# The order of vector and scalar work behind the seven value products, and who forms the rests of one pair's weights

## The chip, the cores and the metric

The kernel runs on one core of a Trainium2 chip. A core has TensorE (PE, matrix products, which land in the accumulation banks "PSUM"), VectorE (DVE), ScalarE (ACT), GpSimd (POOL) and SyncE (SP, which here only issues DMAs). Each engine works through its own queue strictly in order and waits at an instruction until its inputs are there. The metric is the device time of one execution in microseconds, the median of several.

## The reference

A two-layer encoder over 512 tokens of width 1024. The change lies in layer 0, neighbourhood attention on a grid 64 tokens wide:

```python
q, k, v, z = jnp.split(xn @ w_in, 4, axis=-1)      # xn: 512 x 1024, w_in: 1024 x 4096
o = neighbourhood_attention(q, k, v, rpb)          # 16 heads of 64, window 8 x 16, softmax
return (o.reshape(B, S, hd) * jax.nn.silu(z)) @ w_out
```

After it come a gated embedding, layer 1 (latent attention with its own gate) and a final norm. All is float32.

## The kernel before

**Two parts for one number.** A float32 matrix product is made of three passes on rounded parts: an operand is copied by ACT into `whi` (or `xh`, `da`, ...), rounded to the matmul's format, and its rest, operand minus copy, goes into `wlo` (`xl`, `la`, ...). PE then adds hi x hi, hi x lo and lo x hi. A weight of 128 x 1024 (`wraw`, loaded by a DMA that SyncE issues) thus costs one ACT copy and one subtraction, the "rest". `load_w` lets POOL form the rest in one operation of 128 x 1024; `piece` lets DVE form it in two halves of 128 x 512 (`rest`). Both draw on the same rings of three buffers for `wraw`, `whi` and `wlo`.

**Seven products for the values.** `values_seven` computes v = xn @ w_v (512 x 1024 x 1024) by Strassen's scheme in Winograd's form: 2 x 2 blocks and seven products instead of eight, in the order 1, 2, 7, 6, 5, 4, 3. Each product is 24 matmuls of 128 x 512, in two row blocks i = 0, 1 and two depths c = 0, 1, with two weight pieces `W[p][c]`. Products 7, 6, 5, 3 take mixed inputs `V7`, `V6`, `V5`, `V3` (DVE forms the sum into `xT`, ACT its `hi`, DVE its `lo`: `mix`). The mixed weights come from DMAs that add in flight (`W7`, `W5`: `load`) and from sums on DVE (`sums`: `W7` plus a raw piece, in place). Products 5 and 3 add into the banks `C[6]` of product 6, product 4 into the banks `C[7]` of product 7. Between products DVE and ACT combine banks: `after7` adds the saved product 1 (`s1`) to `C[7]` and saves that as `s17`; `after6` saves `C[6]` as `s6` and subtracts it from `C[7]`; `after5` forms the difference of `C[6]` and `s17` and that of `C[6]` and `s1`. `out` splits a finished bank into the tiles `Q` that the attention reads. A bank that is still to be read by a copy or a subtraction cannot be added to by the next product.

**Two head pairs in between.** The query and key projections of head pairs 0 and 1 are set among the seven products (`Pair`): `load` fetches the two weights, `products` runs 2 x 24 matmuls into the "mm" banks, `queries` makes `sa`, `sb` of the first bank, `keys` makes `da`, `db` (ACT) and the rests `la`, `lb` (DVE) of the second, and then the edge copies `s0` on ACT. There are two "mm" banks, so pair 1's products need that `queries(0)` and `keys(0)` have read pair 0's. All later pairs are made by `project`, one before each pair's attention.

**What sets the order.** In this stretch `self.act` and `self.dve` are wrapped in `InOrder`, so that ACT and DVE run in exactly the order in which the lines of `values_seven` stand. PE's value products and pair products are chained likewise. The matmuls of attention heads, of `project` and of all later stages are placed by a planner at build time. POOL and SyncE take their instructions in the planner's order too. Helpers called through `InOrder` are recorded under L51 in the profile.

Of the kernel before, what the change touches and what calls it, by code (L numbers as in the profile page):

```python
# [13 lines left out]
F32 = mybir.dt.float32  # L14
F32R = mybir.dt.float32r
AF = mybir.ActivationFunctionType
ALU = mybir.AluOpType
AX = mybir.AxisListType
PSUM = bass.MemoryType.PSUM
P = 128  # L20
# [36 lines left out]
class Trunk:  # L57
# [189 lines left out]
    def rest(self, hi, lo, raw, o):  # L247
        return self.dve.tensor_tensor(out=lo[:, o], in0=raw[:, o], in1=hi[:, o].bitcast(F32), op=ALU.subtract)
# [18 lines left out]
    def values_seven(self, pool, xT, xk, Q, pair, more):  # L267

        nc = self.nc
        quarter = lambda n, c: self.a["na_v"][n, c:c + 2].rearrange("c p n -> p c n")  # L270
        T = {}

        def load(p, n, c):
            T[p] = pool.tile([P, 2, 1024], F32, name=f"W{p}", bufs=1)
            nc.sync.dma_start(T[p], quarter(1, 0))
            nc.gpsimd.dma_start(T[p], quarter(n, c), accum_op=ALU.add, max_dma_last_dim=4096)

        load(7, 1, 2)
        W, X, C, s1, s17, s6 = {}, {}, {}, {}, {}, {}
        sums = lambda t, i, raw: self.dve.tensor_tensor(out=t[:, i, :], in0=t[:, i, :], in1=raw, op=ALU.add)  # L280

        def left(p, s, k, i):
            if p in X:
                return X[p][:, 2 * s + k // 2, k % 2 * 256 + i * P:k % 2 * 256 + (i + 1) * P]
            half, t = {1: (0, i), 2: (1, i), 4: (1, 2 + i)}[p]
            return xT[s][half][:, k, t * P:(t + 1) * P]

        banks = {1: "SS", 7: "TT", 6: "TO"}
        base = {2: 1, 4: 7, 5: 6, 3: 6}

        def product(p):
            for i in range(2):
                if p in banks:
                    C[p, i] = self.psum(banks[p][i])
            for c, i in [(0, 0), (0, 1), (1, 0), (1, 1)] if p in (1, 2, 7) else [(0, 0), (1, 0), (0, 1), (1, 1)]:
                ps = C[base.get(p, p), i]
                m = [(left(p, s, k, i), W[p][c][r][:, k % 2 * S:(k % 2 + 1) * S])
                     for s, r in ((0, 0), (1, 0), (0, 1)) for k in (2 * c, 2 * c + 1)]
                for j, (l, r) in enumerate(m):
                    with self.tc.issue_after(self.last_mm.ins):  # L300
                        self.last_mm = nc.tensor.matmul(ps, l, r, start=c == 0 and j == 0 and p in banks,  # L301
                                                        stop=c == 1 and j == 5 and p in (2, 3, 4),
                                                        skip_group_check=True)

        sub = lambda o, x, y: self.dve.tensor_tensor(out=o, in0=x, in1=y, op=ALU.subtract)
        kept = lambda name, i: self.temp(name) if name == "s1" or (name, i) == ("s17", 0) else pool.tile([P, S], F32, name=name, tag="s", bufs=3)

        def copy(name, i, ps):
            t = kept(name, i)
            self.act.activation(t, ps, AF.Copy)  # L310
            return t

        def out(th, n, i, ps):
            self.v_split(Q[th, n][:, 2 * i:2 * i + 2, :], ps)

        def after1(i):
            s1[i] = copy("s1", i, C[1, i])

        def after7(i):
            self.dve.tensor_tensor(out=C[7, i], in0=C[7, i], in1=s1[i], op=ALU.add)  # L320
            s17[i] = copy("s17", i, C[7, i])

        def after6(i):
            s6[i] = copy("s6", i, C[6, i])
            sub(C[7, i], C[7, i], s6[i])

        def after5(i):
            q = self.psum("mm")
            sub(q, C[6, i], s17[i])
            sub(C[6, i], C[6, i], s1[i])  # L330
            out(1, 1, i, q)

        made = lambda p, c, raw, vw=False: W.setdefault(p, []).append(self.piece(pool if vw else None, raw)())
        both = range(2)

        def mixed(p):
            X[p], rest = self.mix(xk, p)
            return rest

        made(1, 0, self.raw_piece(0, 0))  # L340
        rest7 = mixed(7)
        made(1, 1, self.raw_piece(0, 1), True)
        load(5, 0, 0)
        rest7()
        made(2, 0, self.raw_piece(0, 2))
        pair.products(0)
        pair.queries(0)
        rest5 = mixed(5)
        product(1)
        after1(0)  # L350
        p21 = self.piece(None, self.raw_piece(0, 3))
        after1(1)
        rest5()
        W[2].append(p21())
        pair.load(1)
        rest6 = mixed(6)
        rest3 = mixed(3)
        rest6()
        rest3()
        more()  # L360
        pair.keys(0)
        made(7, 0, T[7][:, 0, :], True)
        product(2)
        out(0, 0, 0, C[1, 0])
        out(0, 0, 1, C[1, 1])
        made(7, 1, T[7][:, 1, :])
        raws = [self.raw_piece(0, c) for c in both]
        sums(T[7], 0, raws[0])
        made(6, 0, T[7][:, 0, :], True)
        sums(T[7], 1, raws[1])  # L370
        pair.products(1)
        pair.queries(1)
        made(6, 1, T[7][:, 1, :])
        raws = [self.raw_piece(0, 2 + c) for c in both]
        pair.keys(1)
        sums(T[7], 0, raws[0])
        sums(T[7], 1, raws[1])
        made(5, 0, T[5][:, 0, :])
        product(7)
        made(4, 0, T[7][:, 0, :], True)  # L380
        after7(0)
        after7(1)
        made(5, 1, T[5][:, 1, :])
        product(6)
        after6(0)
        after6(1)
        made(4, 1, T[7][:, 1, :], True)
        made(3, 0, self.raw_piece(1, 2))
        product(5)
        made(3, 1, self.raw_piece(1, 3))  # L390
        after5(0)
        after5(1)
        product(4)
        out(1, 0, 0, C[7, 0])
        out(1, 0, 1, C[7, 1])
        product(3)
        out(0, 1, 0, C[6, 0])
        out(0, 1, 1, C[6, 1])

    def na_heads(self, pool, xT, zs, Q, xk, weights, more):  # L400
        nc, a = self.nc, self.a
        A, U = {}, {}
# [18 lines left out]
        def edges(q, last):  # L421
            s0 = []
            for s in q:
                e0 = pool.tile([P, P], F32R, name="s0", tag="s0", bufs=4)
                with self.tc.issue_after(last.ins):
                    self.act.activation(e0.rearrange("p (a b) -> p a b", a=2),
                                        win(s, 0, P, 0, [[448, 2], [1, 64]]).bitcast(F32), AF.Copy)
                s0.append(e0)
            return s0

        def keys(j, psk):
            da = pool.tile([P, S], F32R, name="da", tag="kd", bufs=4)
            db = pool.tile([P, S], F32R, name="db", tag="kd", bufs=4)
            la, lb = self.rest_k[j % 2]
            self.act.activation(da[0:64], psk[0:64], AF.Copy)
            self.act.activation(da[64:128], psk[0:64], AF.Copy)
            self.act.activation(db[64:128], psk[64:128], AF.Copy)
            self.last_key = self.act.activation(db[0:64], psk[64:128], AF.Copy)
            self.dve.tensor_tensor(out=la[0:64], in0=psk[0:64], in1=da[0:64].bitcast(F32), op=ALU.subtract)
            self.dve.tensor_tensor(out=lb[64:128], in0=psk[64:128], in1=db[64:128].bitcast(F32), op=ALU.subtract)  # L440
            return (da, db), (la, lb)

        class Pair:
            ps = {}

            @staticmethod
            def load(j):
                weights[j] = [self.load_w(a["na_qk"][i + j], 1024) for i in (0, 8)]

            @staticmethod  # L450
            def products(j):
# [8 lines left out]
            @staticmethod  # L460
            def keys(j):
                k = keys(j, Pair.ps[j][1])
                A[j] += (edges(A[j][0], self.last_key), *k)

        def project(j):
            wq = self.load_w(a["na_qk"][j], 1024)
            psq = self.psum("mm")
            self.proj_T(psq, wq, xT)
            q = queries(psq)
            wk = self.load_w(a["na_qk"][8 + j], 1024)  # L470
            psk = self.psum("mm")
            last = self.proj_T(psk, wk, xT)
            k = keys(j, psk)
            A[j] = (q, edges(q, self.last_key), *k)
            return last

# [16 lines left out]
        for i in range(2):  # L493
            la = pool.tile([P, S], F32R, name=f"la{i}", bufs=1)
            lb = pool.tile([P, S], F32R, name=f"lb{i}", bufs=1)
# [10 lines left out]
        with self.tc.tile_pool(name="nah", bufs=2, reuse_waits="tile") as hpool:  # L506
            for j in range(8):
                if 0 < j < 7:
                    last = project(j + 1)
                l, step = divmod(j, 4)  # L510
# [948 lines left out]
```

## Time and profile before

| | |
|---|---|
| median of 3 runs | 661.22 us (660.08 to 661.79) |
| the profiled execution | 661.75 us, of which the span of the trace is 660.0 us |
| mean granted clock of TensorE | 0.988 |
| instructions | 9977 |
| POOL's share of the span | 63% |
| DMA | 107.41 MB in all, mean 163 GB/s |

The page cuts the span into 40 slices of 16.5 us, a digit being tenths of a slice in which the engine is busy. The value products run from 55 us to 115 us, that is in slices 4 to 7; the sixteen heads of layer 0 follow up to about 280 us. The profile names tiles without their numbers: `ps_T`, `ps_O`, `ps_S` and `ps_mm` are banks, `s` stands for `s1`, `s17`, `s6` and also for `s0`, `W` for `W7` and `W5`, `V` for all mixed inputs.

### The profile page before, as it was taken

The numbers are of one execution on the slowest core, as the hardware profiler recorded it, in microseconds if no ns is written. First come the engines' busy times: TensorE is split into PE (matmuls) and PEld (weight loads), VectorE is DVE, ScalarE is ACT, GpSimd is POOL, SyncE is SP. The second block draws the span as 40 slices with busy tenths as digits, with TensorE's granted clock in tenths as the row PEclk, the third lists the DMA queues.
The fourth block names the chain that finished last, engine by engine and source line by source line (L and its number), as shares of the span: only waits on it lengthen the run. The fifth ranks groups of instructions, "written<-read, shape, count | busy, mean of one in ns | idle before, by whom it ended". The sixth has DMA issues, their size and how long they took to land.

```text
span 660.0 us, 9977 instructions
## 1 busy us (share of the span) xinstructions
PE 643.6 (98%) x3299; PEld 543.7 (82%) x3299; DVE 430.1 (65%) x882; ACT 454.3 (69%) x903; POOL 413.6 (63%) x373
## 2 busy tenths in 40 slices
PE   9999969999999999999999999999999999999994
PEld 6888848888888888888899888888888888888883
DVE  6197886556666625569834623888888886474675
ACT  7575563888888753587744535888979897537855
POOL 0373101987878764687754625695969887436974
PEclk9999979999999999999999999999999999999998
DMA  9849624787988889545743334220121213573524
GB/s 329 343 136 294 177 95 145 236 216 195 205 261 202 222 140 361 181 129 182 235 121 102 106 108 139 74 77 0 61 62 64 65 65 128 213 297 128 190 65 160
DMA packets 46131, 107.41 MB, mean 163 GB/s; under 512 B 4736, under 2 KB 17792, under 8 KB 46080
## 3 DMA queue, kind: packets, MB, share of 16 engines
q1 hardware_dynamic: 34608, 87.12, 39.2%
q0 software_dynamic: 11040, 18.88, 13.5%
q10 hardware_dynamic: 432, 0.79, 0.3%
q8 instruction: 26, 0.43, 0.3%
q14 instruction: 25, 0.20, 0.1%
HBM read 95.23 MB, written 25.17 MB: 182 GB/s over the span
## 4 chain that ended last, share of the span: by engine, by line
PE 83%; ACT 1%; DVE 0%; issue 0%; POOLq 0%; POOL 0%; DVEq 0%; ACTq 0%
PE ps_mm L123 27%; PE ps_S L123 10%; PE ps_mm L943 7%; PE ps_T L155 6%; PE ps_T L835 5%; PE ps_O L1055 5%; PE ps_mm L835 3%; PE ps_S L835 3%; PE ps_T L301 2%; PE ps_O L592 2%; PE ps_T L123 2%; PE ps_O L123 2%; PE ps_mm L893 2%; PE ps_T L580 1%; PE ps_S L893 1%; PE ps_S L542 1%
## 5 line engine op out<-in xcount | busy, mean ns | idle before, releaser
L101 POOL TENSOR_TENSOR wwlo<-wraw,wwhi 128x1024 fp32r<-128x1024 f32 (+5 forms) x70 | 126.2, 1815 | 99.1 <-ACT wwhi L100 89.1
L780 POOL TENSOR_TENSOR wlo<-wraw,whi 128x512 fp32r<-128x512 f32 x56 | 73.7, 1350 | 23.3 <-ACT whi L778 17.4
L1040 POOL TENSOR_TENSOR ex<-ex,rc 128x512 f32<-128x512 f32 x64 | 66.2, 1043 | 25.9 <-DVE rc L1039 22.3
L100 ACT ACTIVATE wwhi<-wraw 128x1024 fp32r<-128x1024 f32 (+5 forms) x73 | 57.2, 806 | 35.3 <-PE ps_mm L123 16.0
L1038 ACT ACTIVATE ex<-ps_S,mx 128x512 f32<-128x512 f32 x64 | 44.0, 688 | 11.7 <-DVE mx L1036 10.1
L1036 DVE TENSOR_REDUCE mx<-ps_S 128x1 f32<-128x512 f32 x64 | 43.7, 683 | 8.3 <-PE ps_S L123 7.7
L566 POOL TENSOR_TENSOR ex<-ex,rc 128x128 f32<-128x128 f32 (+1 forms) x64 | 37.4, 678 | 18.4 <-DVE rc L562 18.1
L112 DVE TENSOR_TENSOR pt_lo<-ps_T,pt_hi 128x512 fp32r<-128x512 f32 x64 | 43.2, 682 | 7.1 <-ACT pt_hi L110 6.7
L110 ACT ACTIVATE pt_hi<-ps_T 128x512 fp32r<-128x512 f32 x64 | 37.8, 595 | 3.4 <-PE ps_T L155 3.0
L155 PE MATMUL ps_T<-ident,ex 128*128 128x128 f32 x256 | 38.3, 272 | 0.0
L155 PEld LDWEIGHTS ps_T<-ident,ex 128*128 128x128 f32 x256 | 31.5, 140 | 7.5
L221 DVE TENSOR_TENSOR u<-ps_O,u 64x512 f32<-64x512 f32 x32 | 21.9, 686 | 18.2 <-ACT u L220 17.4
L123 PE MATMUL ps_mm<-xh,wwhi 128*128 128x512 f32 x120 | 33.6, 402 | 0.0
L778 ACT ACTIVATE whi<-wraw 128x1024 fp32r<-128x1024 f32 x28 | 29.2, 1055 | 5.8 <-DMA wraw<-sum 3.6
L123 PE MATMUL ps_mm<-xl,wwhi 128*128 128x512 f32 x120 | 32.4, 401 | 0.0
L560 ACT ACTIVATE ex<-ex,mx 128x128 f32<-128x128 f32 (+1 forms) x64 | 30.1, 473 | 2.3 <-DVE mx L549 1.7
L123 PE MATMUL ps_mm<-xh,wwlo 128*128 128x512 f32 x120 | 31.5, 395 | 0.0
L123 PE MATMUL ps_S<-ko,qo 128*128 128x512 f32 x96 | 28.9, 409 | 0.0
L123 PE MATMUL ps_S<-ke,qe 96*128 96x512 f32 x96 | 28.6, 406 | 0.0
L943 PE MATMUL ps_mm<-cT,wwhi 128*128 128x512 f32 x94 | 27.7, 393 | 0.0
L225 POOL TENSOR_TENSOR u<-u,z 128x512 f32<-128x512 f32 x16 | 23.1, 1481 | 4.5 <-DVE u L221 4.5
L123 PEld LDWEIGHTS ps_mm<-xh,wwlo 128*128 128x128 f32 x120 | 22.1, 188 | 4.5
(482 smaller groups left out, 1918.3 us busy)
## 6 DMA issues: line engine op xcount, KB each, us to landing
sum<-gate POOLq DMA_DIRECT2D x12, 1024.0 KB, 9.4
wraw<-na_qk SPq DMA_DIRECT2D x16, 512.0 KB, 4.5
wraw<-sum SPq DMA_DIRECT2D x16, 512.0 KB, 3.3
pe<-pe SPq DMA_DIRECT2D x31, 256.0 KB, 6.6
wraw<-gate SPq DMA_DIRECT2D x12, 512.0 KB, 3.4
wraw<-na_v SPq DMA_DIRECT2D x10, 512.0 KB, 3.4
sum<-sum POOLq DMA_DIRECT2D x4, 1024.0 KB, 11.5
wraw<-na_o SPq DMA_DIRECT2D x8, 512.0 KB, 5.3
```

The source lines that it names most:

```text
L100: nc.scalar.activation(hi[:, c], raw[:, c], AF.Copy)
L101: f = lambda e, c=c: e.tensor_tensor(out=lo[:, c], in0=raw[:, c], in1=hi[:, c].bitcast(F32), op=ALU.subtract)
L110: self.last_copy = self.act.activation(hi, src, AF.Copy, scale=scale)
L112: self.dve.tensor_tensor(out=lo, in0=src, in1=hi.bitcast(F32), op=ALU.subtract)
L123: last = self.last_mm = nc.tensor.matmul(out, l, r, start=i == 0, stop=i == n - 1)
L155: self.last_mm = self.nc.tensor.transpose(t[:, i * P:(i + 1) * P], b, self.ident)
L780: nc.gpsimd.tensor_tensor(out=lo[:, o], in0=raw[:, o], in1=hi[:, o].bitcast(F32), op=ALU.subtract)
L835: mm = nc.tensor.matmul(ps, l, r, start=j == 0 and p in banks, stop=j == 11 and p in (2, 3, 4), skip_group_check=True)
L943: self.last_mm = nc.tensor.matmul(PS[key], *terms[i], start=i == 0, stop=i == len(terms) - 1)
L1036: nc.vector.reduce_max(mx, sp, axis=AX.X, negate=True)
L1038: nc.scalar.activation(ex, sp, AF.Exp, bias=mx, accum_out=sm)
L1040: nc.gpsimd.tensor_tensor(out=ex, in0=ex, in1=rc.to_broadcast([P, S]), op=ALU.mult)
```

## The change

Nothing that is computed changes. Three things move.

1. The weights of head pair 1 are made by `piece`, hence their rests by DVE in four halves at set places of its queue, instead of two operations on POOL. `load` is called once for each weight and gives back the function that forms the rest.
2. In `values_seven` the lines stand in another order: the rests of `keys(0)` and `keys(1)` are called apart from the copies (`rests`); both `sums` of a kind run together; `out(0, 0, ...)`, `keys(1)` and its rests come later; both pieces of W5 are made ahead of `after7`, and `W4`'s first piece behind it.
3. `after5` no longer calls `out(1, 1, i, ...)`; the two calls follow W3's second piece.

```diff
         def after5(i):
-            q = self.psum("mm")
-            sub(q, C[6, i], s17[i])
+            C[5, i] = self.psum("mm")
+            sub(C[5, i], C[6, i], s17[i])
             sub(C[6, i], C[6, i], s1[i])
-            out(1, 1, i, q)
...
         W[2].append(p21())
-        pair.load(1)
+        restq = pair.load(1, 0)
         rest6 = mixed(6)
+        restk = pair.load(1, 8)
+        pair.keys(0)
         rest3 = mixed(3)
+        restq()
         rest6()
+        pair.rests(0)
         rest3()
         more()
-        pair.keys(0)
         made(7, 0, T[7][:, 0, :], True)
         product(2)
+        restk()
+        made(7, 1, T[7][:, 1, :])
+        raws = [self.raw_piece(0, c) for c in both]
+        for c in both:
+            sums(T[7], c, raws[c])
+        for c in both:
+            made(6, c, T[7][:, c, :], not c)
+        raws = [self.raw_piece(0, 2 + c) for c in both]
+        pair.products(1)
+        pair.queries(1)
         out(0, 0, 0, C[1, 0])
         out(0, 0, 1, C[1, 1])
-        made(7, 1, T[7][:, 1, :])
-        raws = [self.raw_piece(0, c) for c in both]
-        sums(T[7], 0, raws[0])
-        made(6, 0, T[7][:, 0, :], True)
-        sums(T[7], 1, raws[1])
-        pair.products(1)
-        pair.queries(1)
-        made(6, 1, T[7][:, 1, :])
-        raws = [self.raw_piece(0, 2 + c) for c in both]
-        pair.keys(1)
-        sums(T[7], 0, raws[0])
-        sums(T[7], 1, raws[1])
+        for c in both:
+            sums(T[7], c, raws[c])
         made(5, 0, T[5][:, 0, :])
         product(7)
-        made(4, 0, T[7][:, 0, :], True)
+        pair.keys(1)
+        made(5, 1, T[5][:, 1, :])
         after7(0)
         after7(1)
-        made(5, 1, T[5][:, 1, :])
+        made(4, 0, T[7][:, 0, :], True)
+        pair.rests(1)
         product(6)
         after6(0)
         after6(1)
         made(4, 1, T[7][:, 1, :], True)
         made(3, 0, self.raw_piece(1, 2))
         product(5)
-        made(3, 1, self.raw_piece(1, 3))
         after5(0)
         after5(1)
+        made(3, 1, self.raw_piece(1, 3))
+        out(1, 1, 0, C[5, 0])
+        out(1, 1, 1, C[5, 1])
         product(4)
...
             def load(j, i):
-                weights[j] = [self.load_w(a["na_qk"][i + j], 1024) for i in (0, 8)]
+                raw = self.wp.tile([P, 1024], F32, name="wraw", tag="wraw", bufs=3)
+                nc.sync.dma_start(raw, a["na_qk"][i + j])
+                rest = self.piece(None, raw)
+                return lambda: weights.setdefault(j, []).append(rest())
```

The first place is DVE between `keys(0)`'s rests and the first additions of `after7`; in the names here W7 and W5 are the mixed weights, `s1` the saved product 1, and a row ending in x2 is a pair of halves. Before:

```order
L51 TENSOR_TENSOR wlo_787<-W7_519,whi_786 128x512 x2
L51 TENSOR_TENSOR la1_512<-ps_mm_731,da_795 64x512
L51 TENSOR_TENSOR lb1_513<-ps_mm_731,db_796 64x512
L51 TENSOR_TENSOR W7_519<-W7_519,wraw_791 128x1024
L51 TENSOR_TENSOR W7_519<-W7_519,wraw_793 128x1024
L51 TENSOR_TENSOR wlo_810<-W5_539,whi_809 128x512 x2
L51 TENSOR_TENSOR wlo_841<-W7_519,whi_840 128x512 x2
L51 TENSOR_TENSOR ps_T_814<-ps_T_814,s1_635 128x512
L51 TENSOR_TENSOR ps_T_815<-ps_T_815,s1_642 128x512
L51 TENSOR_TENSOR wlo_852<-W5_539,whi_851 128x512 x2
```

The same place of DVE in the changed kernel:

```order
L51 TENSOR_TENSOR Q00_679<-ps_S_609,Q00_679 128x4x128
L51 TENSOR_TENSOR Q00_679<-ps_S_610,Q00_679 128x4x128
L51 TENSOR_TENSOR W7_519<-W7_519,wraw_733 128x1024
L51 TENSOR_TENSOR W7_519<-W7_519,wraw_735 128x1024
L51 TENSOR_TENSOR wlo_800<-W5_539,whi_799 128x512 x2
L51 TENSOR_TENSOR wlo_841<-W5_539,whi_840 128x512 x2
L51 TENSOR_TENSOR ps_T_804<-ps_T_804,s1_635 128x512
L51 TENSOR_TENSOR ps_T_805<-ps_T_805,s1_642 128x512
L51 TENSOR_TENSOR wlo_852<-W7_519,whi_851 128x512 x2
L51 TENSOR_TENSOR la1_512<-ps_mm_738,da_830 64x512
L51 TENSOR_TENSOR lb1_513<-ps_mm_738,db_831 64x512
```

The rests of `keys(1)` (`la1`, `lb1`) and of W4's first piece (`W7` minus its copy) moved behind the two additions, W5's second pair ahead of them, and `Q00` further back.

The second place is ACT just before, from the first weight of pair 1 on (`whi_648` before, `whi_649` now; the second is `whi_654`, now `whi_657`). Before:

```order
L100 ACTIVATE wwhi_648<-wraw_647 128x1024
L51 ACTIVATE V6_660<-xT_165 128x1024
L51 ACTIVATE V3_663<-xT_165 128x1024
L51 ACTIVATE da_669<-ps_mm_551 64x512 x2
L51 ACTIVATE db_670<-ps_mm_551 64x512 x2
L51 ACTIVATE s0_677<-sa_600 128x128
L51 ACTIVATE s0_679<-sb_601 128x128
L100 ACTIVATE wwhi_654<-wraw_653 128x1024
L51 ACTIVATE whi_681<-W7_519 128x1024
```

In the changed kernel:

```order
L51 ACTIVATE whi_649<-wraw_647 128x1024
L51 ACTIVATE V6_653<-xT_165 128x1024
L51 ACTIVATE whi_657<-wraw_655 128x1024
L51 ACTIVATE da_660<-ps_mm_551 64x512 x2
L51 ACTIVATE db_661<-ps_mm_551 64x512 x2
L51 ACTIVATE s0_666<-sa_600 128x128
L51 ACTIVATE s0_668<-sb_601 128x128
L51 ACTIVATE V3_671<-xT_165 128x1024
L51 ACTIVATE whi_681<-W7_519 128x1024
```

The second weight's copy now stands ahead of `da` and `db`, and V3's copy behind them.

The third place is PE behind the value products, where `project(2)` (mm banks, query then key weight) leads to the first transposes of the first head (`ident`). Before, from the last scores on; two more matmuls of this query product stand further ahead, within product 3:

```order
L543 MATMUL ps_S_1082<-lb0_509,sb_601 128x256
L123 MATMUL ps_mm_1135<-xh1_159,wwhi_1130 128x512
L123 MATMUL ps_mm_1135<-xl0_160,wwhi_1130 128x512 x4
L123 MATMUL ps_mm_1135<-xl1_161,wwhi_1130 128x512 x4
L123 MATMUL ps_mm_1135<-xh0_158,wwlo_1131 128x512 x4
L123 MATMUL ps_mm_1135<-xh1_159,wwlo_1131 128x512 x4
L123 MATMUL ps_mm_1172<-xh0_158,wwhi_1167 128x512 x4
L123 MATMUL ps_mm_1172<-xh1_159,wwhi_1167 128x512 x4
L123 MATMUL ps_mm_1172<-xl0_160,wwhi_1167 128x512 x4
L123 MATMUL ps_mm_1172<-xl1_161,wwhi_1167 128x512 x2
L578 MATMUL ps_T_1036<-ident_71,ex_1007 128x2x64
```

In the changed kernel, where all 24 matmuls of that query product come behind product 3:

```order
L559 MATMUL ps_S_1084<-lb0_509,sb_601 128x256
L123 MATMUL ps_mm_1137<-xl0_160,wwhi_1132 128x512 x3
L123 MATMUL ps_mm_1137<-xl1_161,wwhi_1132 128x512 x4
L123 MATMUL ps_mm_1137<-xh0_158,wwlo_1133 128x512 x4
L123 MATMUL ps_mm_1137<-xh1_159,wwlo_1133 128x512 x4
L123 MATMUL ps_mm_1174<-xh0_158,wwhi_1169 128x512 x4
L123 MATMUL ps_mm_1174<-xh1_159,wwhi_1169 128x512 x4
L123 MATMUL ps_mm_1174<-xl0_160,wwhi_1169 128x512 x4
L594 MATMUL ps_T_1038<-ident_71,ex_1009 128x2x64
```

The first head's transposes stand two product matmuls earlier in the sequence, and the planner has set PE's sequence over the later heads anew. The order of SyncE's DMAs is the same in both; POOL's list differs, up to the heads, by the two rests that left it.

More of the change, by code (lines that the diff above doesn't have):

```diff
@@ L438, in keys, with key_rests @@
             self.last_key = self.act.activation(db[0:64], psk[64:128], AF.Copy)
-            self.dve.tensor_tensor(out=la[0:64], in0=psk[0:64], in1=da[0:64].bitcast(F32), op=ALU.subtract)
-            self.dve.tensor_tensor(out=lb[64:128], in0=psk[64:128], in1=db[64:128].bitcast(F32), op=ALU.subtract)
             return (da, db), (la, lb)
+        def key_rests(psk, d, l):
+            for t, x, r in ((l[0], d[0], slice(0, 64)), (l[1], d[1], slice(64, 128))):
+                self.dve.tensor_tensor(out=t[r], in0=psk[r], in1=x[r].bitcast(F32), op=ALU.subtract)
         class Pair:
@@ L446, in load @@
             @staticmethod
-            def load(j):
-                weights[j] = [self.load_w(a["na_qk"][i + j], 1024) for i in (0, 8)]
+            def load(j, i):
+                raw = self.wp.tile([P, 1024], F32, name="wraw", tag="wraw", bufs=3)
+                nc.sync.dma_start(raw, a["na_qk"][i + j])
+                rest = self.piece(None, raw)
+                return lambda: weights.setdefault(j, []).append(rest())
             @staticmethod
@@ L463, in keys, with rests @@
                 A[j] += (edges(A[j][0], self.last_key), *k)
+            @staticmethod
+            def rests(j):
+                key_rests(Pair.ps[j][1], *A[j][2:])
         def project(j):
@@ L473, in project @@
             k = keys(j, psk)
+            key_rests(psk, *k)
             A[j] = (q, edges(q, self.last_key), *k)
```

## The prediction

> **What bounds the kernel now.** I read the page first, for the engine that is never free.
>
> ```profile
> span 660.0 us, 9977 instructions
> ...
> PE 643.6 (98%) x3299; PEld 543.7 (82%) x3299; DVE 430.1 (65%) x882; ACT 454.3 (69%) x903; POOL 413.6 (63%) x373
> ...
> PE   9999969999999999999999999999999999999994
> ...
> PEclk9999979999999999999999999999999999999998
> ```
>
> TensorE (PE) is busy 98% of the span, and one of the 40 slices before the last shows a 6 for PE and a 7 for its clock. So work on other engines is worth time only where it makes PE wait. The waits of PE, over the whole span, are next.
>
> ```profile
> PE ps_T L301 <- ACT s L51: 6.3, 1, 6.3
> PE ps_T L1171 <- PEq L1448: 0.8, 1, 0.8
> PE ps_S L123 <- DVE mx L552: 0.2, 1, 0.2
> ```
>
> There is one wait that matters, 6.3 us long, in front of a matmul of a value product (L301) for a copy `s` on ScalarE (ACT). The timeline of PE and the windows around it place it and show its aftermath; the last two windows are the rest of the value products and the attention heads.
>
> ```profile
> 77.57 1.07 PE L301 MATMUL ps_T<-whi,V 128*128 128x512 f32 x4
> ...
> 89.33 0.28 PE L543 MATMUL ps_S<-la,sa 128*128 128x256 f32 x1
> 95.88 2.08 PE L301 MATMUL ps_T<-whi,V 128*128 128x512 f32 x4 [6.28 <-ACT s L51]
> ```
> ```profile
> 89.60:95.88 6.28, 0.00 (x1) 0.00 (x0) 4.64 (x8) 3.12 (x6) 0.00 (x0) 0.66 0.51 167
> 95.88:101.17 5.29, 5.29 (x12) 4.13 (x13) 4.40 (x8) 2.33 (x3) 0.00 (x0) 0.50 0.00 0
> 101.17:104.25 3.08, 3.08 (x14) 2.53 (x12) 0.48 (x1) 1.27 (x2) 0.00 (x0) 0.89 0.49 173
> 104.25:115.60 11.35, 11.35 (x52) 9.40 (x51) 8.29 (x21) 5.03 (x8) 2.80 (x2) 1.00 0.50 163
> 115.60:340.00 224.40, 224.25 (x1208) 193.13 (x1207) 139.50 (x350) 163.55 (x352) 166.53 (x163) 1.00 0.74 208
> ```
>
> Columns are length, busy PE, PEld, DVE, ACT, POOL, then granted clock. Product 7 starts at 77.57, product 6 ends with the first head's scores at 89.6, and PE is idle to 95.88. Then product 5 runs, at clock 0.50 for 5.29 us. Its 24 matmuls take 8.37 us (95.88 to 104.25); at the rate of the 24 of product 4 from 104.25 to 109.69 (5.44) that is 2.93 us lost. The clock averages 0.66 over the idle window: (1 - 0.66)/0.5 x 6.28 = 4.3 us at half, so it fell at 91.6, only 2.0 us after the last matmul. The whole stall costs 6.28 + 2.93 = 9.2 us, the most that this change can win.
>
> What is late? Product 5 adds into the banks that product 6 filled, so it waits until ACT has copied them (`s6`), and these copies stand in ACT's queue behind `s17`, which wait for VectorE (DVE).
>
> ```profile
> 62.48 4.56 DVE L51 TENSOR_TENSOR xT<-xT 128x1024 f32<-128x1024 f32 x2
> 66.96 2.43 DVE L51 TENSOR_TENSOR V<-xT,V 128x1024 fp32r<-128x1024 f32 x2
> 70.47 0.68 DVE L51 TENSOR_TENSOR la<-ps_mm,da 64x512 fp32r<-64x512 f32 x1 [1.07 <-ACT db L51]
> ...
> 72.77 2.65 DVE L51 TENSOR_TENSOR wlo<-W,whi 128x512 fp32r<-128x512 f32 x2 [0.90 <-ACT whi L51]
> 75.45 1.29 DVE L51 TENSOR_TENSOR Q<-ps_S,Q 128x512 fp32r<-128x512 f32 x2
> 76.65 1.28 DVE L51 TENSOR_TENSOR wlo<-W,whi 128x512 fp32r<-128x512 f32 x2
> ...
> 82.66 0.68 DVE L51 SCALAR_TENSOR_TENSOR sa<-ps_mm,sa 64x512 fp32r<-64x512 f32 x1
> ...
> 87.67 2.36 DVE L51 TENSOR_TENSOR W<-W,wraw 128x1024 f32<-128x1024 f32 x2
> 89.95 2.49 DVE L51 TENSOR_TENSOR wlo<-W,whi 128x512 fp32r<-128x512 f32 x4
> 92.47 1.30 DVE L51 TENSOR_TENSOR ps_T<-ps_T,s 128x512 f32<-128x512 f32 x2
> ```
> ```profile
> 61.61 1.06 ACT L100 ACTIVATE wwhi<-wraw 128x1024 fp32r<-128x1024 f32 x1
> ...
> 68.04 1.18 ACT L51 ACTIVATE da<-ps_mm 64x512 fp32r<-64x512 f32 x2
> 69.23 1.20 ACT L51 ACTIVATE db<-ps_mm 64x512 fp32r<-64x512 f32 x2
> ...
> 93.21 1.20 ACT L51 ACTIVATE s<-ps_T 128x512 f32<-128x512 f32 x2 [3.15 <-DVE ps_T L51]
> 94.30 1.05 ACT L51 ACTIVATE whi<-W 128x1024 fp32r<-128x1024 f32 x1
> 95.24 0.59 ACT L51 ACTIVATE s<-ps_T 128x512 f32<-128x512 f32 x1
> ```
>
> Product 7 is complete at 83.0, yet DVE adds into its banks only at 92.47, when everything ahead in its queue is done. That queue, not PE, sets 95.88.
>
> **The change, part by part.** *Rests to DVE.* The two 128x1024 subtractions of the second pair's weights leave POOL and become four halves on DVE. These are POOL's only work in this stretch:
>
> ```profile
> 62.81 3.15 POOL L101 TENSOR_TENSOR wwlo<-wraw,wwhi 128x1024 fp32r<-128x1024 f32 x1 [4.77 <-ACT wwhi L100]
> 71.86 2.40 POOL L101 TENSOR_TENSOR wwlo<-wraw,wwhi 128x1024 fp32r<-128x1024 f32 x1 [5.91 <-ACT wwhi L100]
> ```
>
> DVE pays two pairs of halves, 1.2 us each from start to next start (row 76.65), +2.4. But just while POOL ran those two, DVE was slow: two `xT` took 4.56 where two `V` of one size took 2.43 (2.1 more), and one pair took 2.65 against 1.28 (1.4 more). If POOL's work is the cause, 3.5 us come off, and DVE is 1.1 us better; if not, it is 2.4 worse. I take the first, since both slow rows overlap a POOL row and the undisturbed ones do not.
>
> *Order.* On DVE, ahead of the additions to product 7: four rests for products 6 and 5 as before, the `sa`/`sb` and `Q` rests too; the rests of `keys(1)` (1.4) and of W4's first piece (1.2) go behind them, and DVE's waits for ACT in between shrink. I add up DVE's new queue by these rows, from the same 62.48. Two `xT` 2.4: 64.9. First pair weight's rest 1.2: 66.1. `V6` 1.2: 67.3. Then `la`, `lb` wait for ACT, where the second weight's `whi` now stands ahead of `da`, `db` and waits for its DMA:
>
> ```profile
> 55.73 0.33 SPq L99 DMA_DIRECT2D wraw<-na_qk  x1
> ```
> ```profile
> wraw<-na_qk SPq DMA_DIRECT2D x1, 512.0 KB, 9.5
> ```
> ```profile
> W<-na_v POOLq DMA_DIRECT2D x1, 1024.0 KB, 16.5
> ```
>
> It lands at 55.73 + 9.5 = 65.2; copy 1.05, `da` and `db` 2.4: 68.6. SyncE's queue keeps its order, and the slots that it waits for come free at most 0.2 us later than now, most of them earlier. On DVE `la`, `lb` 1.4: 70.0. `V3` 1.2: 71.3. Three pairs of rests 3.6: 74.9. Two sums 2.3: 77.2. Two pairs 2.4: 79.6. `sa`, `sb` 1.4: 81.0. `Q` 1.2: 82.2. Two sums 2.3: 84.5. W5's two pairs 2.4: 86.9. The two additions end at 88.2 instead of 93.8. On ACT follow the second `s17` (0.6), `whi` of W4 (0.95) and `s6` (0.6): 90.4. So product 5 starts at 90.4, not 95.88: **5.5 us won**. PE, free at 89.6 at the latest, still waits 0.8 to 1.2.
>
> *Clock.* With a gap near 1 us I take the clock as staying full, so product 5 takes 5.44: **2.9 us won**; it ends at 95.8 instead of 104.25. The nearest rows lie on both sides: at full clock no gap over 0.2 us stands within PE's stretch (window 115.60, 224.25 of 224.40 busy), and a gap of 6.28 shut it. Bounds: 0 lost, or as much as now, 2.9. The page "TensorE: Matmul & The Clock Gate" of the Trainium skill (Part 1, What's actually happening) says that the clock falls after at least one idle window of about 3.4 us. By that rule a gap of 1 us keeps the clock full and the sum is 653.3. Here it fell 2.0 us after the last matmul, so the trace does not agree with the rule in its plain form, and I leave the other case a chance.
>
> *Behind product 5.* Product 4 needs, from 95.8 on, the rests of W4's first piece (88.2 or ACT's 89.8, then 1.3: 91.1), `la`, `lb` of the second pair (92.5) and the subtractions of `s6` (93.8); its other half W4's second rest by 97.2 (done 95.0). Product 3 at 101.3 needs C6 after `after5` (97.4 to 98.7) and its last rest (99.9). `out(1, 1)`, moved behind that rest, must free the "mm" banks by 106.7, when `project(2)` starts; it ends near 101. All hidden with 1.3 us or more; if that cover went, PE would wait in front of products 4 or 3 by the excess. POOL's next rest, for `project(2)`, follows ACT's copy at 98.4 and is done by 101. Heads and second layer then keep their places relative to PE, 8.4 us earlier.
>
> **Sum.** The profiled execution took 661.75 (span 660.0 and 1.75 around it), 0.5 above the median of 661.22. 661.75 - 5.5 - 2.9 = **653.3** us. Since most of the run-to-run spread may lie in the stall that goes, I do not lower this to the median's base.
>
> **Rivals.** *The clock still falls.* The gap of 1 us shuts it as that of 6.28 did, and product 5 loses the 2.9 us again: 656.3. For it: 2.0 us sufficed. Against it: half that gap. Chance 0.14.
>
> *DVE stays slow without POOL.* If the 4.56 and 2.65 have another cause, DVE is late by 2.1, of which 1.3 vanish in its wait for `db` (67.3 to 68.6), and by 1.4: product 5 starts 2.2 later, 655.5, or 658.4 if the clock falls too. Against it are the overlaps. Chance 0.10.
>
> *The weight lands late.* ACT waits in front of `da`, `db`. At 16.5 us, the longest landing of this stretch, `whi` starts at 72.2, all of DVE's queue moves by 7.0 and product 5 starts at 97.4. The early pause then lies in front of the second pair's key product, so the clock is full again by product 5, which ends at 102.8, 1.4 before now: 660.3, no change by my bound. Against it: the DMA keeps its place and its 9.5. Chance 0.05.
>
> *Slower: the heads lose their cover.* PE's order is made anew over all 16 heads, with transposes at other places, each behind POOL's normalization.
>
> ```profile
> L566 POOL TENSOR_TENSOR ex<-ex,rc 128x128 f32<-128x128 f32 (+1 forms) x64 | 37.4, 678 | 18.4 <-DVE rc L562 18.1
> ```
> ```profile
> 119.93 2.12 POOL L566 TENSOR_TENSOR ex<-ex,rc 128x128 f32<-128x128 f32 x4
> ```
> ```profile
> 124.72 0.27 PE L578 MATMUL ps_T<-ident,ex 128*128 128x128 f32 x1
> ```
>
> If each head's transposes came one such operation too early, 16 x 0.678 = 10.8 us of new waits: 664.2. It decides from 8.4/16 = 0.53 us a head. For it: POOL is busy 166.5 of 224.4 us there. Against it: PE waits 0.15 us there now, and the first head's transposes come 36 product matmuls behind product 3 as now (two of today's 38 stand ahead of its end), where the normalization is done 2.7 us before them (122.0 and 124.72). Chance 0.05.
>
> **Numbers.** The forecast has 0.66. Faster (by over 0.3%, 2.0 us, about what a measurement of this kernel can tell) is 0.66 + 0.14 + 0.10 = 0.90; same 0.05; slower 0.05. The lower end is the whole stall gone, 661.22 - 9.2 = 652.0, less 0.4 for runs like the fastest; the upper end takes in 656.3 with 0.6 for the half of DVE's case that goes with an open clock. So 651.6 to 656.9, which leaves out late landing, heads and the worse half of DVE's case.
>
> **What would show it.** After: PE's wait at L301 about 1 us, from 89.4 to 90.4; product 5 in 5.4 us, granted clock 1.00 (first step wrong if over 2 us, second if 0.50 appears again); the two `xT` on DVE 2.4 us together and no pair of rests over 1.4; POOL empty from 58 to 98; `da` from 66.3; PE's waits in the heads still under 1 us in sum. I am wrong if another wait of several us stands in front of products 7, 4 or 3, or if the heads show waits in series.

## The result, and the profile after

The changed kernel takes **653.02 us** (652.61 to 653.56, median of 4 runs) beside 660.9 us of the kernel before on the same chip (660.08 to 661.79): ratio 0.9881, 95% interval 0.9864 to 0.9898. The forecast was 653.3. The profiled execution took 653.56, with a span of 651.5.

The page after, its head, then TensorE's 40 slices and its clock:

```profile
span 651.5 us, 9980 instructions
...
PE   9999999999999999999999999999999999999994
...
PEclk9999999999999999999999999999999999999997
```

The 6 and the 7 of the sixth slice are gone. The three largest waits of PE over the whole span, then its timeline at the same place as before:

```profile
PE ps_T L301 <- ACT s L51: 1.2, 1, 1.2
PE ps_T L1187 <- PEq L1464: 0.8, 1, 0.8
PE ps_T L596 <- POOL ex L582: 0.3, 1, 0.3
```
```profile
77.14 1.07 PE L301 MATMUL ps_T<-whi,V 128*128 128x512 f32 x4
...
88.85 0.28 PE L559 MATMUL ps_S<-la,sa 128*128 128x256 f32 x1
90.31 1.21 PE L301 MATMUL ps_T<-whi,V 128*128 128x512 f32 x4 [1.18 <-ACT s L51]
```

The wait in front of product 5 fell from 6.28 to 1.18 us and nothing of its size has come up elsewhere. The windows around it (length, busy PE, PEld, DVE, ACT, POOL, then granted clock) show the second half of the gain; the first is product 5, the last the attention heads:

```profile
90.31:95.92 5.61, 5.61 (x24) 4.61 (x25) 5.54 (x10) 3.39 (x4) 0.00 (x0) 1.00 0.00 0
...
108.00:332.00 224.00, 223.67 (x1210) 193.28 (x1209) 138.37 (x357) 162.81 (x352) 166.23 (x164) 1.00 0.74 209
```

The clock stays at 1.00, so product 5 takes 5.61 us and not 8.37. It starts 5.57 us earlier (95.88 to 90.31) and runs 2.76 us shorter: 8.33 of the 8.5 us by which the span shrank. The timelines of DVE and ACT show how it comes to start earlier:

```profile
62.45 2.48 DVE L51 TENSOR_TENSOR xT<-xT 128x1024 f32<-128x1024 f32 x2
64.84 1.28 DVE L51 TENSOR_TENSOR wlo<-wraw,whi 128x512 fp32r<-128x512 f32 x2
...
68.52 0.68 DVE L51 TENSOR_TENSOR la<-ps_mm,da 64x512 fp32r<-64x512 f32 x1 [1.26 <-ACT db L51]
...
72.29 1.28 DVE L51 TENSOR_TENSOR wlo<-wraw,whi 128x512 fp32r<-128x512 f32 x2
...
86.91 1.29 DVE L51 TENSOR_TENSOR ps_T<-ps_T,s 128x512 f32<-128x512 f32 x2
...
98.56 3.48 DVE L51 TENSOR_TENSOR wlo<-wraw,whi 128x512 fp32r<-128x512 f32 x2
```
```profile
87.63 1.20 ACT L51 ACTIVATE s<-ps_T 128x512 f32<-128x512 f32 x2 [2.49 <-DVE ps_T L51]
88.72 1.05 ACT L51 ACTIVATE whi<-W 128x1024 fp32r<-128x1024 f32 x1
89.67 0.59 ACT L51 ACTIVATE s<-ps_T 128x512 f32<-128x512 f32 x1
```

The two `xT` take 2.48 us instead of 4.56; the second pair's rests (64.84 and 72.29) cost 1.2 us each; the additions of `after7` start at 86.91 instead of 92.47, and `s6` at 89.67 instead of 95.24.

### The profile page after: what moved, and what is told of

Same layout as the page of the kernel before. It is cut to its first block, busy times and chain, and to the rows that moved or that the text cites. A ratio compares the mean times of both kernels' runs of the same rounds, so it can differ in the third digit from the quotient of the medians.

```text
span 651.5 us, 9980 instructions
## 1 busy us (share of the span) xinstructions
PE 640.2 (98%) x3299; PEld 541.9 (83%) x3299; DVE 427.7 (66%) x886; ACT 453.4 (70%) x903; POOL 408.4 (63%) x371
## 4 chain that ended last, share of the span: by engine, by line
PE 83%; POOL 1%; ACT 1%; DVE 0%; DMA 0%; issue 0%; POOLq 0%
PE ps_mm L123 27%; PE ps_S L123 10%; PE ps_mm L959 7%; PE ps_T L155 6%; PE ps_T L851 5%; PE ps_O L1071 5%; PE ps_mm L851 3%; PE ps_S L851 3%; PE ps_O L608 2%; PE ps_T L123 2%; PE ps_O L123 2%; PE ps_mm L909 2%; PE ps_T L301 2%; PE ps_T L596 2%; PE ps_S L909 1%; PE ps_S L559 1%
## 5 line engine op out<-in xcount | busy, mean ns | idle before, releaser
L101 POOL TENSOR_TENSOR wwlo<-wraw,wwhi 128x1024 fp32r<-128x1024 f32 (+5 forms) x68 | 122.3, 1810 | 93.5 <-ACT wwhi L100 41.9
L100 ACT ACTIVATE wwhi<-wraw 128x1024 fp32r<-128x1024 f32 (+5 forms) x71 | 55.1, 799 | 34.3 <-PE ps_mm L123 18.9
L220 ACT ACTIVATE u<-ps_O 64x512 f32<-64x512 f32 x32 | 18.9, 591 | 12.0 <-PE ps_O L608 8.8
```

Source lines behind the costliest of these rows:

```text
L100: nc.scalar.activation(hi[:, c], raw[:, c], AF.Copy)
L101: f = lambda e, c=c: e.tensor_tensor(out=lo[:, c], in0=raw[:, c], in1=hi[:, c].bitcast(F32), op=ALU.subtract)
```

## The experiments

All were timed in rounds against the kernel before on the same chip, five rounds unless said otherwise. Two questions ran through them: how much of the 7.9 us is the order and how much the two rests that left POOL, and when the clock falls.

### x_after: the changed kernel once more

> The changed kernel itself, once more, as the measure for the others of this group on one chip. 653.0 us (seen: 652.6 to 653.6), product 5 from about 90.3 us on.

Measured: 653.19 us (652.28 to 655.46), ratio 0.9886 (0.9868 to 0.9904). The slowest of the four was the profiled one, and it shows something that the first profile did not. ACT, PE and the windows of this execution:

```profile
65.87 1.07 ACT L51 ACTIVATE whi<-wraw 128x1024 fp32r<-128x1024 f32 x1 [1.00 <-DMA wraw<-na_qk]
```
```profile
91.04 1.25 PE L301 MATMUL ps_T<-whi,V 128*128 128x512 f32 x4 [1.81 <-ACT s L51]
```
```profile
91.10:93.00 1.90, 1.90 (x7) 1.52 (x8) 1.89 (x4) 1.90 (x3) 0.00 (x0) 0.75 0.00 0
93.00:97.00 4.00, 4.00 (x14) 3.20 (x13) 3.94 (x8) 0.72 (x2) 0.00 (x0) 0.69 0.00 0
```

The second key weight landed later, ACT's copy of it held `da` and `db` up, all of DVE's queue moved, and the gap grew to 1.81 us. Then the clock fell, although PE was already running again. Of the eight executions of this kernel on record it alone has a mean clock of 0.994; the others have 0.995 to 0.997. Its half clock cost less than the rival "the clock still falls" had put on it: product 5 took 7.17 us (91.04 to 98.21), 1.6 more than 5.61, and began 0.73 later.

### a_pool: the new order, the rests back on POOL

```diff
-                rest = self.piece(None, raw)
-                return lambda: weights.setdefault(j, []).append(rest())
+                hi, lo = (self.wp.tile([P, 1024], F32R, name=t, tag=t, bufs=3) for t in ("whi", "wlo"))
+                self.act.activation(hi, raw, AF.Copy)
+                nc.gpsimd.tensor_tensor(out=lo, in0=raw, in1=hi.bitcast(F32), op=ALU.subtract)
+                return lambda: weights.setdefault(j, []).append((hi, lo))
```

> The new order with the second pair's two rests back on GpSimd. Theory 'the order does it all, and the move to VectorE is paid for': the first GpSimd operation slows the two xT sums by 2.1 us, of which 1.3 vanish in VectorE's wait for db, the second falls mostly into that wait, and 2.4 us of rests leave VectorE's queue: it is 1.0 us ahead of the changed kernel, product 5 starts at 89.3, the gap shrinks to 0.2, and the time is 652.0 us. Rival, the prediction's account (3.5 us of slowing against 2.4 us of rests): 1.1 us behind, product 5 at 91.4, 654.1 us.

Measured: 654.34 us (654.04 to 654.59), ratio 0.9898 (0.9885 to 0.9912). DVE and POOL of this run:

```profile
62.47 4.56 DVE L51 TENSOR_TENSOR xT<-xT 128x1024 f32<-128x1024 f32 x2
66.95 3.42 DVE L51 TENSOR_TENSOR V<-xT,V 128x1024 fp32r<-128x1024 f32 x1
70.39 0.68 DVE L51 TENSOR_TENSOR la<-ps_mm,da 64x512 fp32r<-64x512 f32 x1
```
```profile
62.80 3.15 POOL L460 TENSOR_TENSOR wlo<-wraw,whi 128x1024 fp32r<-128x1024 f32 x1 [4.93 <-ACT whi L51]
66.50 2.79 POOL L460 TENSOR_TENSOR wlo<-wraw,whi 128x1024 fp32r<-128x1024 f32 x1 [0.55 <-PE ps_S L301]
```

As soon as POOL has the two rests again, the two `xT` take 4.56 and the one `V` beside the second rest 3.42 instead of 1.22. The price against the changed kernel: 2.08 + 2.20 for the slowing, less 2.4 for two pairs of rests, less the 1.26 that DVE otherwise stands waiting for `db`: 0.62. `after7` starts 0.66 later (87.57). My first theory, that the second POOL operation would fall into DVE's idle time, missed: it fell on `V` in full.

### b_dve: the old order, the rests on DVE

The edit gives the kernel before the new `load`, and calls the two rests behind V3's `mixed` and, behind `keys(0)`, after W7's first piece.

> The old order, only the second pair's two rests on VectorE. Theory (VectorE's queue sets the start of product 5): the slowing by GpSimd goes, which is worth more than the rests cost here, since VectorE then stops less for ScalarE: product 5 at 93.0 instead of 95.9, the clock still falls in the gap of 3.8 us: 658 us. Rival, the move without the order brings nothing: 661 us.

Measured: 659.3 us (658.17 to 659.66), ratio 0.9969 (0.9958 to 0.998). DVE's two `xT` and PE's wait:

```profile
62.35 2.48 DVE L51 TENSOR_TENSOR xT<-xT 128x1024 f32<-128x1024 f32 x2
```
```profile
PE ps_T L301 <- ACT s L51: 4.4, 1, 4.4
```

More work on DVE, and `after7` nonetheless starts at 90.10, 2.4 us earlier than before. By medians the move alone is worth 1.7 us, the order alone 6.7 (a_pool), both 7.8 to 7.9. That the two add up to 0.5 more than both together is not explained by a run: the clock, which falls in the old order and not in the new, is in these numbers too. b_dve's two executions with a mean clock of 0.993 took 658.2 and 658.6, its four with 0.990 or 0.991 took 659.1 to 659.7.

### c_late: the old order, with two rests put behind after7

Only W4's first piece and the rests of `keys(1)` move behind the additions of `after7`.

> The kernel before with only the last part of the new order: W4's first piece and the rests of keys(1) behind the additions to product 7 (GpSimd keeps its two rests, W5's second piece stays behind the additions). Theory (VectorE's queue sets product 5): 2.6 us leave the queue ahead of the additions, but two weight copies, not one, now stand between s17 and s6 on ScalarE: product 5 at 94.1 instead of 95.9, clock still falling: 659.1 us. Rival, that this is the part that matters: 654 us or less.

Measured: 659.25 us (657.62 to 660.25), ratio 0.9971 (0.9961 to 0.9982). ACT of this run says why product 5 starts only 2.6 us earlier than before (93.30) when `after7` starts 3.5 us earlier (88.94):

```profile
90.76 1.99 ACT L51 ACTIVATE whi<-W 128x1024 fp32r<-128x1024 f32 x2
92.65 0.59 ACT L51 ACTIVATE s<-ps_T 128x512 f32<-128x512 f32 x1
```

In front of `s6` there now stand two copies `whi` (W5's and W4's) where there was one, 0.95 us more, and the clock still fell. By medians the gain is 1.9 us, so most of the order's 6.7 lies in the rest of it, and part of that is the clock, which a_pool kept. Which move of the rest brings how much, no run separates.

### d_next and f_land: what is left of the wait

d_next puts W5's second pair of rests behind `after7`, and the other work of that place behind both `s6`. f_land loads the second key weight at its place, but copies it behind `da`, `db` and V3:

```diff
-        restk = pair.load(1, 8)
         pair.keys(0)
         rest3 = mixed(3)
+        restk = pair.load(1, 8)
         restq()
         rest6()
         pair.rests(0)
         rest3()
         more()
+        restk()
         made(7, 0, T[7][:, 0, :], True)
         product(2)
-        restk()
```

> The changed kernel with W5's second pair of rests behind the additions to product 7, and W4's first piece, the rests of keys(1) and the subtractions behind both copies s6. VectorE is 1.2 us earlier at the additions, s6 comes at 88.5, product 5 at 89.2, right behind the scores: the remaining gap of 1.2 us goes. 651.9 us. Rival: W5's second rest, done at 89.8, or the subtractions, done at 94.4, are now late for products 5 and 4, and the wait only moves: 653 us.

> The changed kernel with one thing moved: the copy of the second pair's key weight, which waits for its DMA (65.2 us), stands behind da, db and V3's copy on ScalarE, and its rest ahead of W7's first. Theory (VectorE's only idle time in this queue is its wait of 1.3 us for db, and that is the wait for this DMA): la starts at 67.3 instead of 68.5, product 5 at 89.1, the gap of 1.2 us goes: 651.8 us, and the slower executions go with it. Rival: db is late for another reason, 653.0 us.

Measured: d_next 652.44 us (652.01 to 652.68), ratio 0.9869 (0.9854 to 0.9884); f_land 652.5 (652.15 to 652.6), ratio 0.9868 (0.9855 to 0.9881). PE at the start of product 5 in f_land, and DVE there:

```profile
88.86 1.19 PE L301 MATMUL ps_T<-whi,V 128*128 128x512 f32 x4
```
```profile
67.06 0.68 DVE L51 TENSOR_TENSOR la<-ps_mm,da 64x512 fp32r<-64x512 f32 x1
```

Neither has a wait in front of product 5 (d_next starts it at 89.00); in f_land `la` no longer waits for `db` at all. Only 0.37 us of DVE's 1.26 us wait for `db` in the changed kernel was ACT standing still ahead of the second weight's copy; the rest was the copy itself in front of `da` and `db`, so f_land's theory names under a third of what it removed. Both spans (650.4 and 650.3) are 1.1 to 1.2 shorter than that of the changed kernel's profile, which is the wait that it showed; between the medians it is 0.5 to 0.8, both came out 0.5 to 0.7 above their numbers, and the intervals of the ratios overlap with the changed kernel's. The likely reason is that the median execution of the changed kernel has a shorter gap than its profiled one: g1, below, shows an execution in which DVE waited 0.77 for `db` instead of 1.26. f_land's runs lie within 0.45 us of each other and d_next's within 0.67, those of x_after within 3.2. d_next keeps the weight's copy in its place, so the narrow runs come with the missing gap and do not single out the landing.

### h_both: the two together

> The changed kernel with the edits of d_next and f_land together. If what is left after the change is only the wait ahead of product 5 (0.6 us over the median), each of the two edits has already taken all of it, and both together give 652.4 us, the same as either alone (652.44 and 652.5), with no wait of TensorE over 0.4 us in the value products. Rival: the two gains are of different things and add, 651.9 us.

Measured: 651.89 us (651.72 to 652.04), ratio 0.9864 (0.985 to 0.9877), the lowest median of all versions. The largest waits of PE in h_both, then in d_next:

```profile
PE ps_T L1189 <- PEq L1466: 0.8, 1, 0.8
```
```profile
PE ps_mm L675 <- ACT whi L654: 0.8, 1, 0.8
...
PE ps_T L301 <- ACT Q L51: 0.2, 1, 0.2
PE ps_S L123 <- DVE mx L570: 0.2, 1, 0.2
```

The number is the rival's, but not for its reason, since neither part had a gap left to give. What d_next's execution has over h_both's is a wait of 0.8 us at the kernel's start, which g3's has too, and one of 0.2 ahead of product 3; its span is 0.5 longer. The intervals of the three ratios overlap, so that half microsecond is not established.

### g1 and g3: a longer gap on purpose

One (g1) and three (g3, `range(3)`) extra copies on ACT (a mixed weight onto itself) ahead of `s6`, 0.95 us each.

```diff
+        for i in range(1):
+            self.act.activation(T[5][:, 0, :], T[5][:, 0, :], AF.Copy)
```

> The changed kernel with one more copy of 128x1024 on ScalarE in front of s6 (0.95 us), so that PE's gap before product 5 is 2.1 us. Theory of windows: the clock falls for 3.4 us when PE was idle for about half of one of the fixed windows of 3.4 us; the gap lies at random in them, so some executions (about 6 in 10) lose another 1.7 us and the rest do not: times in two groups near 654.0 and 655.7. Rival, only a gap of a whole window counts: all near 654.0. Rival, any gap of 2 us shuts it: all near 655.7.

> The changed kernel with three more ScalarE copies of 0.95 us ahead of s6, so that TensorE stands still for about 4 us ahead of product 5 in every execution. If a gap shuts the clock by where it lies in windows of 3.4 us, a gap of 4 us always shuts it: 653.0 + 2.9 for the longer gap + 1.7 to 2.9 for the half clock = 657.6 to 658.8 us, and the half clock lasts 3.41, 6.83 or 10.24 us. Rival: the clock falls only for a gap as long as that of the kernel before (6.28 us), 655.9 us at a clock that stays full.

Measured: g1 654.77 us (653.06 to 656.98; the runs 653.06, 653.24, 654.35, 655.2, 656.53, 656.98), ratio 0.9905 (0.9887 to 0.9923); g3 657.65 (656.98 to 658.46), ratio 0.9949 (0.9936 to 0.9963). PE of g1's profiled execution (653.24), then PE and windows of g3's:

```profile
90.87 1.21 PE L301 MATMUL ps_T<-whi,V 128*128 128x512 f32 x4 [1.65 <-ACT s L51]
91.92 0.62 PE L301 MATMUL ps_T<-wlo,V 128*128 128x512 f32 x2
```
```profile
93.16 2.08 PE L301 MATMUL ps_T<-whi,V 128*128 128x512 f32 x4 [4.07 <-ACT s L51]
```
```profile
92.00:94.00 2.00, 0.84 (x2) 0.75 (x3) 0.99 (x3) 2.00 (x4) 0.00 (x0) 0.54 0.00 0
94.00:96.00 2.00, 2.00 (x6) 1.52 (x6) 1.86 (x4) 1.48 (x2) 0.00 (x0) 0.50 0.00 0
```

In g1 the profiled execution kept its clock after a gap of 1.65 us (the next two matmuls after the first four take 0.62, not 1.05), and the six runs spread over 3.9 us instead of falling into the two tight groups that I expected. Their mean clocks, in the order of the times, are 0.996, 0.996, 0.996, 0.997, 0.992 and 0.993: the clock fell in the two slowest only, and what made 654.35 and 655.2 longer at a full clock is not shown. In g3 the median is where the first theory put it, and the mean clock of all five runs is 0.991 to 0.994; in the profiled one it was at half for about 6.8 us. A gap of 4.07 us is enough; the gap of before was not needed.

### e_pool: more work for POOL beside DVE

Fourteen subtractions of 128x342 on POOL, whose result nobody reads, run beside DVE's queue; three rounds.

> The changed kernel with 14 subtractions of 128x342 on GpSimd, into a tile that nothing reads, from about 65 to 77 us, that is beside VectorE's queue. Theory (GpSimd slows VectorE's operations with two inputs in SBUF, by 0.7 us for each us of GpSimd): V6, V3, three pairs of rests and a sum come 6 us later in all, 1.3 of it in the wait for db; product 5 at about 95, the clock falls: about 660 us, with pairs of rests of 2.5 us or more in the trace. Rival, the slow rows of the kernel before had another cause: 653.0 us and pairs of 1.3 us.

Measured: 662.66 us (661.81 to 663.48), ratio 1.0021 (1.0012 to 1.003). All of the change's gain is gone, though nothing waits for POOL's work here; the time is even 2.7 us above the number expected, and product 5 starts at 97.81 instead of 95. DVE, POOL and the largest wait of PE:

```profile
68.60 0.68 DVE L51 TENSOR_TENSOR la<-ps_mm,da 64x512 fp32r<-64x512 f32 x1
...
71.40 2.74 DVE L51 TENSOR_TENSOR wlo<-W,whi 128x512 fp32r<-128x512 f32 x2
...
79.38 3.82 DVE L51 TENSOR_TENSOR W<-W,wraw 128x1024 f32<-128x1024 f32 x2
```
```profile
66.25 19.05 POOL L361 TENSOR_TENSOR spare<-V 128x342 f32<-128x342 f32 x13
```
```profile
PE ps_T L301 <- ACT s L51: 6.3, 1, 6.3
```

While POOL runs, a pair of rests takes 2.74 instead of 1.28 and two sums 3.82 instead of 2.35. That is the contention which the prediction inferred from overlaps, made at will.

## Why the prediction was right

**Order.** The new queue of DVE, summed row by row, put the end of `after7`'s additions at 88.2; the trace has 86.91 + 1.29 = 88.20. It put `s6` done and product 5 started at 90.4; the trace has 90.26 and 90.31. The wait that was to stay, 0.8 to 1.2, is 1.18. a_pool shows that this term is the bulk, and c_late that the last part of the order alone does not bring it. d_next does without one part of it, W5's second rest ahead of `after7`.

**Rests to DVE.** The choice that DVE's slow rows came from POOL held: b_dve, a_pool and e_pool show it from three sides, and the rival "DVE stays slow without POOL" falls. The price of the move within the new order was not separated in the prediction: it named 1.1 us of DVE's time; a_pool has 0.66 us of it on the path, or 1.15 to 1.3 by medians.

**Clock.** Right for the profiled execution and, by times and mean clocks, for seven of eight, with 2.76 won instead of 2.9. The reason given, that the gap is short enough, holds for the gap forecast: one of 1.18 us leaves PE busy for at least 2.23 of any 3.41 us around it, and the last section finds no fall after a window as busy as that. What the prediction lacked is that the gap varies. x_after's 655.46 lies near the rival's 656.3, but not by the rival's mechanism: it was a gap of 1.81 us and not of 1, so the 0.14 is not tested by it.

**Behind product 5.** No wait, as said, but not by the sum given. PE is busy from 91 to 108 throughout, and in the heads for 223.67 of 224.00 us: the one new wait there is 0.3. W3's second rest, however, was put at 98.7 to 99.9, while the same paragraph has POOL forming a rest from 98.4 to 101. The slowing that the prediction charged elsewhere was left out here: the pair took 3.48 us and ended at 102.04, which also breaks the sign "no pair of rests over 1.4". That is later than the 101.3 at which the prediction has product 3 need it. PE did not wait because product 3, from 101.36 on, first reads the second piece's rest at 103.63. So the sum's zero stands, and the margin named for this rest does not. POOL's rest and those first matmuls in the changed kernel:

```profile
98.58 2.91 POOL L101 TENSOR_TENSOR wwlo<-wraw,wwhi 128x1024 fp32r<-128x1024 f32 x1 [40.80 <-PE ps_T L301]
```
```profile
103.63 0.62 PE L301 MATMUL ps_T<-wlo,V 128*128 128x512 f32 x2
```

**Sum.** From profile to profile the gain is 8.2 of the 8.4 forecast, from median to median 7.9. The base was the profiled execution because the spread was expected to go with the stall; x_after spreads over 3.2 us where the kernel before spreads over 1.7. From the median the same sum gives 652.8, as near, so the choice did not decide it.

**The weight lands late.** Priced with its worst landing, which did not occur; a small one did: in x_after ACT waited 1.00 us for the DMA. It is the one traced cause of a slow execution; whether it makes most of the changed kernel's spread is not shown.

## What to carry to other kernels

When one engine is busy throughout and another feeds it in strict order, write that feeder's queue out row by row with durations from undisturbed rows, and ask of every slow row what ran on GpSimd at that time: taking work from a mostly idle GpSimd can make VectorE finish earlier. After the large wait has gone, remove the last microsecond as well: it is worth little in the median (0.5 to 1.3 us here), but none of the twelve executions of d_next, f_land and h_both took over 652.7 us, while one of the changed kernel's eight took 655.46 with a gap that also cost the clock.

## What the runs showed of the hardware

**VectorE and GpSimd seem to take turns where VectorE reads both inputs from SBUF.** In a_pool one addition of 128x1024 took 3.42 us instead of 1.22 (`V`), while GpSimd's rests of 128x1024 took 3.15 and 2.79, beside 2.40 in an undisturbed row. The ends fit an operation that waits until the other engine's is over: GpSimd's two rests end at 65.95 and 69.29, and VectorE's second `xT` and `V` at 67.03 and 70.37, each 1.08 later. So the loss is no fixed factor but goes by how much of the other engine's operation is still to come. Operations with an input from a bank are spared: `la` took 0.68 in e_pool as everywhere. The Trainium skill, page "GPSIMD Engine Reference", section 1, states an interface shared with VectorE, with contention where VectorE has two SBUF inputs; the traces agree, and show what it costs here.

**The clock went by windows of 3.41 us, and by how busy PE was in the one just over.** Six profiled executions here fell to half clock at product 5. Cut at the moment of the fall, each reads alike; the kernel before and x_after, first the window ahead of the fall, then those behind it:

```profile
88.22:91.63 3.41, 1.38 (x7) 0.92 (x5) 3.41 (x5) 1.06 (x1) 0.00 (x0) 1.00 0.47 149
91.63:95.04 3.41, 0.00 (x0) 0.00 (x0) 2.11 (x4) 1.83 (x3) 0.00 (x0) 0.50 0.46 159
95.04:98.46 3.42, 2.58 (x6) 2.09 (x7) 3.08 (x6) 3.17 (x5) 0.00 (x0) 0.50 0.00 0
98.46:101.87 3.41, 3.41 (x9) 2.64 (x9) 1.82 (x4) 0.00 (x0) 0.00 (x0) 0.50 0.05 7
101.87:105.28 3.41, 3.41 (x16) 2.81 (x16) 1.51 (x3) 2.12 (x2) 0.10 (x1) 1.00 0.40 149
```
```profile
88.64:92.05 3.41, 1.60 (x9) 1.25 (x9) 1.80 (x4) 3.41 (x6) 0.00 (x0) 1.00 0.07 29
92.05:95.46 3.41, 3.41 (x9) 2.64 (x8) 3.33 (x6) 1.32 (x2) 0.00 (x0) 0.50 0.00 0
95.46:98.88 3.42, 3.42 (x16) 2.82 (x15) 3.20 (x6) 2.23 (x3) 0.00 (x0) 1.00 0.15 22
```

| | PE busy in the 3.41 us ahead of the fall | in the windows at half clock | half clock lasts |
|---|---|---|---|
| before | 1.38 | 0.00, 2.58, 3.41 | 10.24 |
| e_pool | 1.30 | 0.00, 2.62, 3.41 | 10.24 |
| c_late | 1.16 | 1.98, 3.42 | 6.83 |
| g3 | 0.34 | 2.41, 3.42 | 6.83 |
| b_dve | 0.13 | 3.41 | 3.41 |
| x_after | 1.60 | 3.41 | 3.41 |

The windows keep their place through an execution. In each of the twelve profiled executions all changes of the clock lie whole numbers of 3.413 us apart, however far: before's fall at 91.63 and the one near its end at 654.83 by 165 of them. So the windows can also be laid over the executions that kept their clock at product 5:

| | gap | PE busy in the windows that hold it |
|---|---|---|
| a_pool | 1.49 | 1.93 |
| after | 1.18 | 2.23 |
| g1 | 1.65 | 2.56, 2.61 |

Over all windows at full clock in the twelve executions, it fell after every one with PE busy for 1.60 us or less, and after none with 1.93 or more; what decides in between, no window here shows. In all six it came back at the end of the first window in which PE was busy throughout, and a window busy for 2.62 of 3.41 was not enough. So where a gap lies counts as well as its length: a_pool's 1.49 us within one window left 1.93, x_after's 1.81 left 1.60, and g1's 1.65 was split between two. This is read from the records after the fact: no run was made to test it. The Trainium skill, page "TensorE: Matmul & The Clock Gate", Part 1, has a fall after at least one idle window of about 3.4 us: the length agrees with 3.41, but PE need not have been idle for all of it.
